# A decoder trunk in fp32 on one core: six seven-product pairs per feed-forward duo, and low parts of two down units by accumulating DMA

## The chip, the core and the metric

The kernel runs on one core of a Trainium2 chip. Its engines each work off a list of their own in order: PE (the matmul engine, with PEld loading its stationary operand), DVE, ACT, POOL and SP, and DMA queues move data between HBM and the on-chip memory. Engines wait for each other by semaphores. The metric is the device time of one launch in microseconds. The kernel before takes 2178.19 us, the median of three runs (2178.04 to 2179.07). Below, "us" is microseconds, and L followed by a number is a line of kernel.py; "before" and "changed" differ in line numbers, since the change adds lines (L294 and L296, the two halves of a split, become L314 and L316; L317 becomes L348; L423 becomes L469; L370 to L372 become L416 to L418; L445 to L447 become L491 to L493; L1129, L1133 and L1203 become L1179, L1183 and L1254).

## The reference

The reference is a two-layer decoder: a gated linear attention mixer, a feed-forward, a shared K/V projection, a differential attention and a second feed-forward, all in float32 on x of 256 tokens by 2048. The change touches the feed-forward alone, which runs twice with D_FF = 5632:

```python
def swiglu(h, w_gate_up, w_down):
    gate, up = jnp.split(h @ w_gate_up, 2, axis=-1)
    return (jax.nn.silu(gate) * up) @ w_down

f = swiglu(rmsnorm(x, pre_ffn_g[i]), ffn_w_gate_up[i], ffn_w_down[i])
x = x + rmsnorm(f, post_ffn_g[i])
```

## The kernel before, in words

**Float32 by three products.** Every weight streams in once, in units of 128 x 1024 floats (512 KB), by DMAs on SP's queue into five buffers called `raw`. A unit is then split into two parts that TensorE multiplies at its fast rate: ACT casts it to `hi` (L294), and DVE subtracts, `lo = raw - hi` (L296). Activations are held as such pairs too. A product of two 128 x 128 by 128 x 512 blocks is three matmuls of 128 x 512: high by high, high by the weight's low, low by the weight's high (`mm_act`, L370 to L372, and `triple`, L445 to L447). There are nine pairs of `hi` and `lo` buffers. A `raw` buffer comes free once its unit is split, and the next load then starts.

**The feed-forward.** Gate and up have 11 chunks of 512 columns each. Gate chunk c is worked together with up chunk 11 + c, as a "duo": eight steps over the contraction (s = 0 to 7), each of which brings four 128 x 512 blocks of weights for two contraction tiles, times two blocks of tokens, so eight products. For some steps the kernel uses a scheme with seven products in place of eight (a "seven-product pair" below), after Strassen: sums of the weights' blocks and of the activations' blocks are multiplied, and the duo's results are put together from seven PSUM banks. Its price is four additions of the raw weights on DVE (`sums`, L317), after which three whole units (kinds a, b, c) and one half unit (kind d, in narrow buffers) are split. An "ordinary pair" splits two units. The tuple FAST_FFN names the steps with seven products: (0, 2, 3, 4, 6); duo 1 uses (0, 2, 4, 6); chunk 0 runs without any.

After the last seven-product step of a duo, `early` takes four banks apart (a copy on ACT, L1140, and four operations on DVE, L1129); at step 7 `late` adds the remaining banks, applies silu on ACT (L1151) and multiplies gate by up on DVE (L1133). The gated chunk is transposed on PE and split again (`split_T`, L609 to L612) before the down projection can use it.

**The down runs.** The down projection works on groups of chunks, FF_GROUPS = ((0, 1), (2, 3), (4, 5), (6, 7), (8,), (9, 10)). After a duo comes a run of eight down units (four contraction steps for two column chunks), each of 12 matmuls; group (2, 3) for example gives one run for output chunks 0 and 1 after duo 3, and one for 2 and 3 after duo 4. A run starts its PSUM banks from the sum so far (a copy on ACT, L423), and a finished bank is copied back by ACT (`evac`, L1203). These copies stand in ACT's list among the casts.

**What sets the order.** The code asks for units in the order of a stream; `pump` converts units ahead of the step that takes them, as far as the buffers allow. A scheduler then orders each engine's list by its own estimate of times, unless an `issue_after` or a priority tells it otherwise.

Of the kernel before, what the change touches and what calls it, by code (L numbers as in the profile page):

```python
# [11 lines left out]
F32 = mybir.dt.float32  # L12
# [10 lines left out]
C = 512  # L23
# [16 lines left out]
FAST_MIX = (0, 2, 4, 6)  # L40
FAST_FFN = (0, 2, 3, 4, 6)
FAST_SECOND = (0, 2, 4, 6)
FAST_OUT = (0, 2, 3, 5)
FAST_V = (0, 2, 4, 5)
SKEW, LAST_SKEW = 7, 8
CHAIN = (3, 4, 5, 6)
FIRST_X = {1: [(1, 0), (0, 1)], 3: [(1, 1)], 5: [(0, 2)], 7: [(1, 2)], 9: [(0, 3)], 11: [(1, 3)]}
NRAW, NRING = 5, 9
V_BEGIN, V_EVERY, V_Q = 16, 3, 1


def ffn_pairs(c):

    return FAST_SECOND if c == 1 else FAST_FFN

# [78 lines left out]


def load_list(stream):
    out = []
    for name, idx, kind in stream:
        if kind in ("plain", "beside"):
            out.append((name, idx))  # L140
        elif kind == "a":
            out.extend((name, (n, idx[2])) for name, n in idx[:2])
    return out
# [43 lines left out]
class Trunk:  # L187
    def __init__(self, ctx, tc, t):
        self.ctx, self.tc, self.nc, self.t = ctx, tc, tc.nc, t

        def pool(name, **kw):
            return ctx.enter_context(tc.tile_pool(name=name, bufs=1, **kw))

        self.const = pool("const")
        self.big = pool("big")
        self.ring = pool("ring")
        self.hs = pool("hs")
        self.psum = pool("psum", space=bass.MemoryType.PSUM)
        self.dram = pool("dram", space=bass.MemoryType.DRAM)
        self.n = 0  # L200
        self.later = []
        self.stream = weight_stream()
        self.loads = load_list(self.stream)
        self.n_used = self.n_done = 0
        self.subs = {}
        self.raws = {}
        self.n_dma = self.n_conv = self.n_take = self.n_free = 0
        self.pool_lo = set()
        self.n_narrow = 0
        self.cap = 2  # L210
        self.ident = self.const.tile([P, P], F32, tag="ident", name="ident")
# [78 lines left out]
    def split(self, src, gp=False):  # L290
        nc = self.nc
        w = src.shape[-1]
        hi, lo = self.places(w)
        nc.scalar.copy(hi, src)  # L294
        eng = nc.gpsimd if gp else nc.vector
        eng.tensor_tensor(out=lo, in0=src, in1=hi.bitcast(F32), op=ALU.subtract)  # L296
        return hi, lo
# [27 lines left out]
    def convert(self):  # L325
# [3 lines left out]
        if kind == "plain":  # L329
            self.subs[n] = self.split(self.raw(), n in self.pool_lo) if n else self.split_halves(self.raw())  # L330
        elif kind == "beside":
# [17 lines left out]
    def take(self, name, idx, kind="plain"):  # L349
# [3 lines left out]
        self.pump()  # L353
        return self.subs.pop(n)

    def free(self):
# [92 lines left out]
    def duo_act(self, aT, forms, fast, c1, c2, early, late):  # L449

        ps = [self.acc() for _ in range(6)] + [self.tp().rearrange("p j t -> p (j t)")]
        for s in range(8):
            k1, k2 = 2 * s, 2 * s + 1
            if s in fast:
# [18 lines left out]
                if last:  # L473
                    early(ps)
                continue
            for (w, n), pair in ((c1, ((1, 0), (3, 1))), (c2, ((4, 1), (2, 2)))):
                wp = self.take(w, (n, s))
                for bank, which in pair:
# [3 lines left out]
                    if s == 7:  # L482
                        late(bank, ps)
                    if bank in (2, 3):
# [3 lines left out]
    def duo_apart(self, aT, forms, fast, chunks, early, late):  # L488
# [9 lines left out]
        for s in range(8):  # L498
            k1, k2 = 2 * s, 2 * s + 1
            if s not in fast:  # L500
                for (w, n), banks in zip(chunks, ((1, 3), (2, 7))):
                    wp = self.take(w, (n, s))
                    for b, bank in enumerate(banks):
# [4 lines left out]
                        if s == 7:  # L508
                            late(bank, ps)
                        self.tick()  # L510
# [15 lines left out]
            if last:  # L526
                early(ps)

# [631 lines left out]
    def ffn(self, fp, hT, rs, gi, wgu, wd, post, after, name, reload, side=None):  # L1160
        nc = self.nc
        self.narrow, self.n_narrow = (fp, 0, 3), 0
        forms = Forms(FAST_FFN, range(8), self.whole(4, [P, 4, 2, 4, P], f"{name}_fast", F32R))
# [9 lines left out]
        def gate_T(sg, c):  # L1173
# [3 lines left out]
            for b in range(2):  # L1177
                self.split_T(gTs[grp], 4 * grp.index(c), sg[:, b, :], b)

# [35 lines left out]
        for n, (kind, which, *chunks) in enumerate(plan):  # L1215
# [21 lines left out]
            def done(c, b, ps, grp=which):  # L1237
                (self.urgent(evac) if skew else evac)(grp, c, b, ps)

# [347 lines left out]
```

## Time and profile before

| | before |
|---|---|
| runs, median (lowest to highest) | 2178.19 us (2178.04 to 2179.07) |
| the profiled execution, its own time | 2178.21 us |
| its span, first to last instruction | 2176.5 us |
| PE busy | 2161.2 us (99%), 10098 matmuls |
| DVE busy | 1889.5 us (87%) |
| ACT busy | 1341.4 us (62%) |
| POOL busy | 36.3 us (2%) |
| DMA | 440.09 MB, mean 202 GB/s |
| mean granted TensorE clock | 0.999 |

The profile is of one execution. Its busy rows give each engine's busy time over the whole span; a row of a group of instructions reads "line, engine, operation, out<-in, shapes, count | busy us, mean ns of one | idle time of the engine just before them, and what ended most of it". A row of the timeline reads "start us, duration us, engine, line, operation, ...", with a wait in brackets. A row of the table of waits reads "engine, what it was about to write, its line <- the engine and line that released it: us in all, times, the longest". A matmul's own duration (0.39 us) overlaps the next one's, so its price is read from the distance between starts.

### The profile page before, as it was taken

What the parts mean: (1) busy time and instruction counts of PE and PEld (TensorE: products, weight loads), DVE (VectorE), ACT (ScalarE), POOL (GpSimd) and SP (SyncE); (2) the same over time, 40 slices, a digit from 0 to 9 for tenths busy, and PEclk for the clock granted to TensorE, in tenths of its full rate; (3) what the DMA queues carried; (4) which work ended last, traced back from release to release, by engine and by line L of the source; (5) the groups of instructions that cost most, each with busy time, mean ns of one, the idle gap of its engine ahead of it and who ended that gap; (6) DMA issues with size and microseconds to landing.
All of it is one profiled execution on the core that took longest, in us unless ns stands there. A gap on an engine that the chain in (4) does not pass through costs nothing.

```text
span 2176.5 us, 28464 instructions
## 1 busy us (share of the span) xinstructions
PE 2161.2 (99%) x10098; PEld 1797.6 (83%) x10098; DVE 1889.5 (87%) x2566; ACT 1341.4 (62%) x1888; POOL 36.3 (2%) x66
## 2 busy tenths in 40 slices
PE   9999999999999999999999999999999999999998
PEld 7887788888888888888788888888888888888886
DVE  7989988999899989988798567889998999899985
ACT  8656655666656666666676455556566666666664
POOL 1000000000000000000000000000000000000000
PEclk9999999999999999999999999999999999999999
DMA  8546566667655566565757655465656556566664
GB/s 309 168 150 191 176 228 212 215 212 246 204 179 193 198 213 212 195 222 191 239 189 245 189 172 164 149 233 195 230 197 221 189 178 197 204 209 220 204 212 136
DMA packets 123315, 440.09 MB, mean 202 GB/s; under 512 B 13899, under 2 KB 16628, under 8 KB 121380
## 3 DMA queue, kind: packets, MB, share of 16 engines
q1 hardware_dynamic: 121996, 436.44, 60.2%
q10 hardware_dynamic: 1176, 1.84, 0.2%
q8 instruction: 79, 1.29, 0.2%
q14 instruction: 64, 0.52, 0.1%
HBM read 429.82 MB, written 9.97 MB: 202 GB/s over the span
## 4 chain that ended last, share of the span: by engine, by line
PE 98%; DVE 1%; issue 0%; DMA 0%; ACT 0%; POOL 0%; SPq 0%; DVEq 0%; POOLq 0%; ACTq 0%
PE acc L445 13%; PE acc L447 13%; PE acc L446 13%; PE acc L372 11%; PE acc L370 11%; PE acc L371 11%; PE acc L588 8%; PE acc L589 4%; PE tp L445 3%; PE tp L446 3%; PE tp L447 3%; PE tp L609 1%; DVE lo L296 1%; PE acc L1310 0%; PE acc L1349 0%; PE tp L644 0%
## 5 line engine op out<-in xcount | busy, mean ns | idle before, releaser
L294 ACT CAST hi<-raw 128x1024 fp32r<-128x1024 f32 x905 | 929.7, 1051 | 568.2 <-DVE raw L317 227.2
L296 DVE TENSOR_TENSOR lo<-raw,hi 128x1024 fp32r<-128x1024 f32 x903 | 1079.6, 1219 | 182.2 <-ACT hi L294 179.4
L371 PE MATMUL acc<-lo,f_ffn_gT 128*128 128x512 f32 x704 | 273.7, 389 | 0.0
L370 PE MATMUL acc<-hi,f_ffn_gT 128*128 128x512 f32 x704 | 273.1, 390 | 0.0
L372 PE MATMUL acc<-hi,f_ffn_gT 128*128 128x512 f32 x704 | 268.5, 389 | 0.0
L445 PE MATMUL acc<-hi,h_ffn 128*128 128x512 f32 x666 | 259.3, 389 | 0.0
L447 PE MATMUL acc<-hi,h_ffn 128*128 128x512 f32 x666 | 259.3, 389 | 0.0
L446 PE MATMUL acc<-lo,h_ffn 128*128 128x512 f32 x666 | 259.1, 389 | 0.0
L372 PEld LDWEIGHTS acc<-hi,f_ffn_gT 128*128 128x128 f32 x704 | 132.2, 188 | 27.4
L370 PEld LDWEIGHTS acc<-hi,f_ffn_gT 128*128 128x128 f32 x704 | 132.0, 188 | 27.5 <-issue 0.6
L371 PEld LDWEIGHTS acc<-lo,f_ffn_gT 128*128 128x128 f32 x704 | 132.2, 188 | 27.1
L447 PEld LDWEIGHTS acc<-hi,h_ffn 128*128 128x128 f32 x666 | 125.0, 188 | 26.0
L446 PEld LDWEIGHTS acc<-lo,h_ffn 128*128 128x128 f32 x666 | 125.1, 188 | 25.9
L445 PEld LDWEIGHTS acc<-hi,h_ffn 128*128 128x128 f32 x666 | 125.0, 188 | 25.8
L588 PE MATMUL acc<-h_q,hi 128*128 128x512 f32 x256 | 92.6, 402 | 0.0
L588 PE MATMUL acc<-h_kv,hi 128*128 128x512 f32 x256 | 90.6, 399 | 0.0
L588 PE MATMUL acc<-h_mix,hi 128*128 128x512 f32 x256 | 90.6, 398 | 0.0
L317 DVE TENSOR_TENSOR raw<-sum,raw 128x512 f32<-128x512 f32 x122 | 84.3, 691 | 3.8
L317 DVE TENSOR_TENSOR raw<-raw 128x512 f32<-128x512 f32 x122 | 84.3, 691 | 3.6
L317 DVE TENSOR_TENSOR raw<-raw,raw 128x512 f32<-128x512 f32 x122 | 83.9, 687 | 2.3
L1203 ACT COPY f_ffn<-acc 128x512 f32<-128x512 f32 x80 | 46.9, 586 | 60.8 <-PE acc L372 60.6
L317 DVE TENSOR_TENSOR sum<-raw,raw 128x512 f32<-128x512 f32 x122 | 83.4, 684 | 0.0
(412 smaller groups left out, 3966.1 us busy)
## 6 DMA issues: line engine op xcount, KB each, us to landing
raw<-in_w_gu_dram SPq DMA_DIRECT2D x352, 512.0 KB, 4.5
raw<-in_w_d_dram SPq DMA_DIRECT2D x176, 512.0 KB, 4.9
raw<-in_gla_w_r_dram SPq DMA_DIRECT2D x32, 512.0 KB, 4.7
raw<-in_gla_w_v_dram SPq DMA_DIRECT2D x32, 512.0 KB, 4.0
raw<-in_gla_w_out_dram SPq DMA_DIRECT2D x32, 512.0 KB, 4.5
raw<-in_w_v_dram SPq DMA_DIRECT2D x32, 512.0 KB, 4.5
raw<-in_w_k_dram SPq DMA_DIRECT2D x32, 512.0 KB, 4.5
raw<-in_diff_w_q_dram SPq DMA_DIRECT2D x32, 512.0 KB, 4.2
```

Source lines behind the costliest of these rows:

```text
L294: nc.scalar.copy(hi, src)
L296: eng.tensor_tensor(out=lo, in0=src, in1=hi.bitcast(F32), op=ALU.subtract)
L317: nc.vector.tensor_tensor(out=out, in0=in0, in1=in1, op=ALU.add)
L370: nc.tensor.matmul(ps, ah, rh, start=(kt == 0 and not onto), stop=False, skip_group_check=onto)
L371: nc.tensor.matmul(ps, ah, rl, start=False, stop=False, skip_group_check=onto)
L372: nc.tensor.matmul(ps, al, rh, start=False, stop=(kt == 2 * ns - 1), skip_group_check=onto)
L445: nc.tensor.matmul(ps, ah, wh, start=first, stop=False)
L446: nc.tensor.matmul(ps, ah, wl, start=False, stop=False)
L447: nc.tensor.matmul(ps, al, wh, start=False, stop=last)
L588: nc.tensor.matmul(ps, lh, aT.both(kt), start=(kt == 0), stop=False)
L589: nc.tensor.matmul(ps[:, SEQ:], ll, aT.hi(kt), start=False, stop=(kt == KT - 1))
L1203: nc.scalar.copy(fc, ps)
```

## The change

Three things change in the feed-forwards.

- Steps with seven products: duos 2 to 9 get six of them, (0, 2, 3, 4, 5, 6); duo 10 keeps five, now (0, 2, 3, 5, 6); duo 1 keeps four. The forms of the activations for the sixth are built with the others, and half units now have two narrow buffers of their own and two places beside the activations' forms, where they had three such places.
- In each run of eight down units, units 6 and 7 are split without DVE: ACT writes the negated unit into `lo`, a DMA issued by POOL loads the unit from HBM once more and adds it to what stands in `lo`, and ACT casts `hi`. The buffer `lo` is of the same rounded type as `hi`, so that what ACT writes there is the negated high part, and the sum is the low part, raw - hi. There are 22 such units in each feed-forward.
- `early` and `late` of a duo are ordered, by the context manager `behind`, after the cast and the subtraction of the last unit that is converted up to three ahead of the one being taken.

```diff
-FAST_FFN = (0, 2, 3, 4, 6)
+FAST_FFN = (0, 2, 3, 4, 5, 6)
 FAST_SECOND = (0, 2, 4, 6)
+FAST_LAST = (0, 2, 3, 5, 6)
...
+DOWN_LO_BY_DMA, DUO_LO_BY_DMA = (6, 7), ()
+EARLY_BEHIND, LATE_BEHIND, DOWN_BEHIND, GATE_BEHIND = 3, 3, 0, 0
...
-    return FAST_SECOND if c == 1 else FAST_FFN
+    return FAST_SECOND if c == 1 else FAST_LAST if c == 10 else FAST_FFN
...
+def lo_by_dma(stream):
+
+    out, last, run = set(), None, 0
+    for n, (name, idx, kind) in enumerate(stream):
+        run = run + 1 if (name, kind) == last else 0
+        last = name, kind
+        if kind != "plain":
+            continue
+        if name in ("w_d0", "w_d1") and run % 8 in DOWN_LO_BY_DMA:
+            out.add(n)
...
+        cast = nc.scalar.copy(hi, src)
+        eng = nc.gpsimd if gp else nc.vector
+        rest = eng.tensor_tensor(out=lo, in0=src, in1=hi.bitcast(F32), op=ALU.subtract)
+        if not gp:
+            self.parts[self.n_conv] = cast.ins, rest.ins
+        return hi, lo
+
+    def split_by_dma(self, src, name, idx):
+
+        nc = self.nc
+        hi, lo = self.places(2 * C)
+        nc.scalar.activation(lo, src, AF.Copy, scale=-1.0)
+        nc.gpsimd.dma_start(lo, self.t[name][idx], accum_op=ALU.add)
         nc.scalar.copy(hi, src)
-        eng = nc.gpsimd if gp else nc.vector
-        eng.tensor_tensor(out=lo, in0=src, in1=hi.bitcast(F32), op=ALU.subtract)
         return hi, lo
...
+            if n in self.dma_lo:
+                self.subs[n] = self.split_by_dma(self.raw(), name, idx)
...
+    @contextmanager
+    def behind(self, ahead):
+
+        made = [n for n in self.parts if n < self.n_take + ahead]
+        if not made or not ahead:
+            yield
+            return
+        cast, rest = self.parts[max(made)]
+        with self.tc.issue_after(cast), self.tc.issue_after(rest):
+            yield
...
                 if last:
-                    early(ps)
+                    with self.behind(EARLY_BEHIND):
+                        early(ps)
...
                         if s == 7:
-                            late(bank, ps)
+                            with self.behind(LATE_BEHIND):
+                                late(bank, ps)
...
-        self.narrow, self.n_narrow = (fp, 0, 3), 0
+        self.narrow, self.n_narrow = (fp, 2, 2), 0
```

The scheduler reorders the lists around this. Three places show it, all of the first feed-forward; numbers behind names count up as the program is built. The first is DVE's list at the end of duo 5 and the start of the run of down units behind it. `lo_6384` and `lo_6396` before, `lo_6471` and `lo_6483` in the change, are the two units of the duo's last ordinary pair; the rows behind them are the run's units, and L1129 (L1179) is `early` and `late`. Before:

```order
L296 TENSOR_TENSOR lo_6441<-raw_6367,hi_6440 128x1024
L296 TENSOR_TENSOR lo_6453<-raw_6387,hi_6452 128x1024
L296 TENSOR_TENSOR lo_6465<-raw_6399,hi_6464 128x1024
L296 TENSOR_TENSOR lo_6477<-raw_6408,hi_6476 128x1024
L1129 TENSOR_TENSOR hs_6492<-acc_6234,sg_6491 128x512
L296 TENSOR_TENSOR lo_6486<-raw_6426,hi_6485 128x1024
L1129 TENSOR_TENSOR sg_6491<-tp_6203,hs_6492 128x512
L1129 TENSOR_TENSOR sg_6491<-acc_6182,sg_6491 128x512
```

In the change:

```order
L316 TENSOR_TENSOR lo_6471<-raw_6367,hi_6470 128x1024
L316 TENSOR_TENSOR lo_6483<-raw_6401,hi_6482 128x1024
L316 TENSOR_TENSOR lo_6495<-raw_6413,hi_6494 128x1024
L1179 TENSOR_TENSOR hs_6568<-acc_6297,sg_6567 128x512
L316 TENSOR_TENSOR lo_6507<-raw_6445,hi_6506 128x1024
L1179 TENSOR_TENSOR sg_6567<-tp_6266,hs_6568 128x512
L316 TENSOR_TENSOR lo_6516<-raw_6457,hi_6515 128x1024
L1179 TENSOR_TENSOR sg_6567<-acc_6245,sg_6567 128x512
L316 TENSOR_TENSOR lo_6528<-raw_6474,hi_6527 128x1024
L1179 TENSOR_TENSOR hs_6569<-acc_6278,sg_6567 128x512
```

Before, six units of the run are split ahead of the first operation of `early` (`lo_6405` to `lo_6477`); in the change one is (`lo_6495`), and the four operations stand between the splits of the next ones.

The second place is ACT's list, at the last units of that run and, further on, at the copies of the finished down sums. Before:

```order
L294 CAST hi_6513<-raw_6444 128x1024
L1151 ACTIVATE sg_6491<-sg_6491,rs_ffn_0_3744 128x512
L423 COPY acc_6600<-f_ffn_4427 128x512
L294 CAST hi_6535<-raw_6456 128x1024
...
L294 CAST hi_6668<-raw_6517 128x1024
L1203 COPY f_ffn_4427<-acc_6541 128x512
L294 CAST f_ffn_rest<-sum_6684 128x512
L294 CAST hi_6689<-raw_6566 128x1024
L1203 COPY f_ffn_4427<-acc_6542 128x512
L294 CAST hi_6709<-raw_6517 128x1024
```

In the change:

```order
L325 ACTIVATE lo_6561<-raw_6510 128x1024
L327 CAST hi_6560<-raw_6510 128x1024
L469 COPY acc_6678<-f_ffn_4440 128x512
L325 ACTIVATE lo_6590<-raw_6519 128x1024
L327 CAST hi_6589<-raw_6519 128x1024
L314 CAST hi_6612<-raw_6531 128x1024
...
L314 CAST hi_6747<-raw_6594 128x1024
L1254 COPY f_ffn_4440<-acc_6618 128x512
L1254 COPY f_ffn_4440<-acc_6677 128x512
L1254 COPY f_ffn_4440<-acc_6619 128x512
L314 CAST hi_6768<-raw_6643 128x1024
L314 CAST hi_6802<-sum_6763 128x512
```

Units 6 and 7 of the run (`raw_6510`, `raw_6519`) have two rows each where a unit had one, and `hi_6612` is the first cast of the next duo. `hi_6689` before and `hi_6768` in the change are the same unit, kind b of the next duo's pair 2: one copy of a down sum stands ahead of it before, three stand ahead of it now.

The third place is PE's list in duo 6, at step 5 (names in `f_ffn_rest` are the activations' forms of the later pairs). Before it is an ordinary pair, and the three matmuls of a product stand in a row:

```order
L445 MATMUL acc_6719<-hi_6837,h_ffn_1_3490 128x512
L446 MATMUL acc_6719<-lo_6838,h_ffn_1_3490 128x512
L447 MATMUL acc_6719<-hi_6837,h_ffn_1_3490 128x512
L445 MATMUL acc_6741<-hi_6837,h_ffn_1_3490 128x512
L446 MATMUL acc_6741<-lo_6838,h_ffn_1_3490 128x512
L447 MATMUL acc_6741<-hi_6837,h_ffn_1_3490 128x512
```

In the change it is a seven-product pair, and several matmuls with `hi` stand ahead of the first with `lo`:

```order
L491 MATMUL tp_6806<-hi_6933,f_ffn_rest 128x512
L491 MATMUL acc_6810<-hi_6933,f_ffn_rest 128x512
L491 MATMUL acc_6837<-hi_6957,f_ffn_rest 128x512
L492 MATMUL tp_6806<-lo_6934,f_ffn_rest 128x512
L493 MATMUL tp_6806<-hi_6933,f_ffn_rest 128x512
L492 MATMUL acc_6810<-lo_6934,f_ffn_rest 128x512
L493 MATMUL acc_6810<-hi_6933,f_ffn_rest 128x512
```

The step has 21 matmuls where it had 24. The scheduler's order also differs in the steps around it; each unit's `hi` is asked for a few matmuls earlier than its `lo`.

More of the change, by code (lines that the diff above doesn't have):

```diff
@@ L1 @@
 import math
-from contextlib import ExitStack
+from contextlib import ExitStack, contextmanager
 import numpy as np
@@ L133, in weight_stream @@
     return out
+def lo_by_dma(stream):
[7 more added lines that the diff above has]
+            out.add(n)
+        if name in ("w_gu0", "w_gu1") and idx[0] % 11 > 1 and idx[1] in DUO_LO_BY_DMA:
+            out.add(n)
+    return out
 def load_list(stream):
@@ L205, in __init__ @@
         self.subs = {}
+        self.parts = {}
         self.raws = {}
@@ L208, in __init__ @@
         self.pool_lo = set()
+        self.dma_lo = lo_by_dma(self.stream)
         self.n_narrow = 0
@@ L329, in convert @@
         if kind == "plain":
-            self.subs[n] = self.split(self.raw(), n in self.pool_lo) if n else self.split_halves(self.raw())
+            name, idx, _ = self.stream[n]
+            if n in self.dma_lo:
+                self.subs[n] = self.split_by_dma(self.raw(), name, idx)
+            else:
+                self.subs[n] = self.split(self.raw(), n in self.pool_lo) if n else self.split_halves(self.raw())
         elif kind == "beside":
@@ L508, in duo_apart @@
                         if s == 7:
-                            late(bank, ps)
+                            with self.behind(LATE_BEHIND):
+                                late(bank, ps)
                         self.tick()
@@ L526, in duo_apart @@
             if last:
-                early(ps)
+                with self.behind(EARLY_BEHIND):
+                    early(ps)
     def rest_of(self, forms, i, name):
@@ L1177, in gate_T @@
             for b in range(2):
-                self.split_T(gTs[grp], 4 * grp.index(c), sg[:, b, :], b)
+                with self.behind(GATE_BEHIND):
+                    self.split_T(gTs[grp], 4 * grp.index(c), sg[:, b, :], b)
         def new_sg():
@@ L1237, in done @@
             def done(c, b, ps, grp=which):
-                (self.urgent(evac) if skew else evac)(grp, c, b, ps)
+                if skew:
+                    self.urgent(evac)(grp, c, b, ps)
+                else:
+                    with self.behind(DOWN_BEHIND):
+                        evac(grp, c, b, ps)
             base = None if which == first else part
```

## The prediction

> **What bounds the kernel now.** I read the page's busy shares and its chain first, then the waits of PE, then a busy table over one repeating stretch of the feed-forward, then that stretch row by row.
>
> ```profile
> PE 2161.2 (99%) x10098; PEld 1797.6 (83%) x10098; DVE 1889.5 (87%) x2566; ACT 1341.4 (62%) x1888; POOL 36.3 (2%) x66
> ...
> PE 98%; DVE 1%; issue 0%; DMA 0%; ACT 0%; POOL 0%; SPq 0%; DVEq 0%; POOLq 0%; ACTq 0%
> ```
> ```profile
> PE acc L372 <- DVE h_kv L650: 2.8, 2, 2.3
> ```
> ```profile
> 560.62:686.17 125.55, 125.55 (x565) 104.17 (x563) 114.56 (x132) 78.01 (x95) 0.00 (x0) 1.00 0.61 201
> 686.17:811.72 125.55, 125.55 (x564) 104.17 (x563) 114.45 (x132) 78.03 (x95) 0.00 (x0) 1.00 0.60 201
> ```
> The chain is PE for 98% of the span, and the longest entry in the list of PE's waits is 2.8 us, outside the feed-forward. The two windows (stretch, us, then busy us of PE, weight load, DVE, ACT, POOL) are two periods of one feed-forward, each of two duos and two runs of eight down units: PE is busy for all of each 125.55 us at a granted clock of 1.00, so matmuls alone set the time. DVE is the next engine: 114.45 of 125.55 us, 11.1 us idle per period, 5.5 us per duo with its run.
>
> A busy PE may be waiting on nothing and still run below its peak, so the price of a matmul is read from starts:
>
> ```profile
> 708.20 0.39 PE L446 MATMUL acc<-lo,f_ffn_fast 128*128 128x512 f32 x1
> 708.43 0.39 PE L447 MATMUL acc<-hi,f_ffn_fast 128*128 128x512 f32 x1
> 708.65 0.39 PE L445 MATMUL acc<-hi,h_ffn 128*128 128x512 f32 x1
> 708.88 0.39 PE L446 MATMUL acc<-lo,h_ffn 128*128 128x512 f32 x1
> ```
> Three steps in 0.68 us: 0.2267 us per matmul. A product of three matmuls costs 0.68 us, a seven-product pair 4.76, an ordinary pair 8 x 0.68 = 5.44, a down unit (12 matmuls) 2.72.
>
> **What the change removes from PE.** Eight duos in each of two feed-forwards get one more seven-product pair, each with one product less: 16 x 3 = 48 matmuls, 48 x 0.2267 = 10.9 us. It is all on the path that sets the end, as long as the operands arrive. That condition is the whole question, because it is DVE that pays.
>
> **What it adds to DVE.** The price of a pair on DVE, from starts where DVE has no gap:
>
> ```profile
> 688.80 0.68 DVE L317 TENSOR_TENSOR raw<-raw,raw 128x512 f32<-128x512 f32 x1
> ...
> 695.58 0.69 DVE L317 TENSOR_TENSOR raw<-raw,raw 128x512 f32<-128x512 f32 x1
> ...
> 699.98 4.62 DVE L296 TENSOR_TENSOR lo<-raw,hi 128x1024 fp32r<-128x1024 f32 x4
> ...
> 709.05 5.76 DVE L296 TENSOR_TENSOR lo<-raw,hi 128x1024 fp32r<-128x1024 f32 x5
> ```
> From the first sum of one seven-product pair to that of the next, 695.58 - 688.80 = 6.78 us: four sums, three splits of a whole unit, one of a half. Five splits in a row take 5.76 us, 1.15 each, so an ordinary pair costs 2.3. One pair converted adds 4.5 us. In the down run two of eight units lose their split: -2.3. Net +2.2 us per duo with its run: 57.2 (half of 114.45) becomes 59.4 us, while PE's 62.8 becomes 62.1. The margin shrinks from 5.5 to 2.7 us. Over the program that is 16 x 4.5 - 44 x 1.15 = +21 us of DVE (44 units, 22 in each feed-forward), and some 5 us for the two sixth forms, in the first chunks, where all units are ordinary. DVE would be 96% used in a period, so the average fits; the lead within the duo has to be looked at.
>
> **The lead.** In a seven-product pair PE gains 6.78 - 4.76 = 2.02 us on DVE, in an ordinary pair DVE gains 5.44 - 2.3 = 3.1, in a down unit 1.57. The split at 699.98 (the last whole one of pair 4, over at 701.20) is read at 708.20: a lead of 7.0 us. The one at 709.05 (pair 6, over at about 710.3) is first read here:
>
> ```profile
> 718.40 0.39 PE L446 MATMUL acc<-lo,f_ffn_rest 128*128 128x512 f32 x1
> ```
> a lead of 8.1. With pair 5 converted, this second lead falls by 3.1 + 2.02 to 3.0 us if DVE comes into the duo as far ahead as now, and the two spared splits could add 2.3: at best 5.3. At worst DVE comes in later. What limits its lead at the duo's start is ACT, in order:
>
> ```profile
> 744.43 0.59 ACT L1203 COPY f_ffn<-acc 128x512 f32<-128x512 f32 x1 [4.34 <-PE acc L372]
> ```
> A copy of a finished down sum stands between the casts for the next pairs and waits 4.34 us for PE; DVE waits behind it. In the new order three such copies stand ahead of the casts of pair 2 in one kind of run and two in the other. Counting matmuls in the new order from the duo's last ordinary pair, PE ends the last of these sums at 29.0 or 28.1 us; copy, cast and split (0.59, 1.05, 1.22, and 0.35 I allow for signals) bring pair 2's second unit to 32.2 or 31.3, and PE reads it at 40.8 or 38.7: a lead of 8.6 or 7.4. From there to the same unit of pair 6 PE takes 19.5 or 21.5 us (60.27 less these; the new order runs some first matmuls ahead of the low part's), DVE 4 x 6.78 = 27.1, and 1.3 more for a gate's split in the second kind. Left: 1.0 or 0.5 us. I go by this end, since ACT's order is what the row shows, and the reckoning is good to about 1.2 us. So a duo in four may wait, about 0.2 us each on the mean: 16 x 0.2 = 3 us. If DVE's cover is gone altogether, it is the second rival.
>
> **The evacuations** move behind the first down unit's split. DVE's four operations of some 0.6 us then stand among the splits of the run, where DVE now has gaps; the sums that PE needs for the run's first chunks are freed by the first of them. Nothing, while the lead holds; up to 0.6 us per run if a sum comes late. This is inside the 1.2 us.
>
> **The low parts by DMA.**
>
> ```profile
> L294 ACT CAST hi<-raw 128x1024 fp32r<-128x1024 f32 x59 | 60.6, 1050 | 36.9 <-DVE raw L317 25.3 <-DMA raw<-in_w_d_dram 6.0 <-issue 2.6
> ```
> ```profile
> raw<-in_w_d_dram SPq DMA_DIRECT2D x176, 512.0 KB, 4.9
> ```
> ACT gets a negated copy per unit (priced as its cast, 1.05), 2.1 us per run, and with the converted pair 1.05 + 0.62 more: 39.0 of 62.8 us becomes 42.8 of 62.1. It stays off the path. POOL issues 44 DMAs, where it has nothing queued in these stages; the norms' small operations behind the last two come after PE's last sums anyway. The DMA engines are busy 0.60 and get 44 x 0.52 = 23 MB on 440. The trace has no accumulating DMA. Below, it costs a plain load, 4.9 us; above, twice that with the destination read, plus the issue on POOL, about 11. What it may take: unit 6's own load follows the release by unit 1's split (about 3 us into the last pair), lands 4.9 later, so the negated copy ends near 9 to 10; PE first reads the low part at 20.1 or 22.9 by the count. About 10 us are free, so I price it at nothing, with the upper end just touching.
>
> [...]
>
> **Sum.** The profiled execution took 2178.21 us (span 2176.5, 1.7 around it), as good as the median of 2178.19. 2178.2 - 10.9 = 2167.3; + 3 for thin leads = **2170 us**.
>
> **Rivals.** (1) *Part of the gain is eaten by DVE*: the lead runs out in every duo, by 0.3 to 0.9 us, 5 to 14 us in all: 2172 to 2181, say 2175. For it: the lead of 0.5 to 1.0. Against: DVE's gaps of now (8.9 us a period are waits for casts) shrink when it is late.
>
> ```profile
> DVE lo L296 <- ACT hi L294: 8.9, 13, 1.8
> ```
> (2) *DVE becomes the bound*, slower than before. If DVE keeps all of its 5.5 us of gaps per duo, it needs 59.4 + 5.5 = 64.9 us, 2.1 over the present 62.8: 16 x 2.1 = +34, 2212; it decides above 3.4 us of gaps, half way 2195. For: the four ACT operations of the two units stand ahead of the next duo's first cast. Against: gaps that come from waiting for PE go when PE is not behind. (3) *The accumulating DMA lands late*, above some 10 us from the negated copy: each microsecond more costs one in each of 22 runs; at 12 us 2170 + 44 = 2214. [...] (4) *The saving is not there*: PE's removed products turn into waits of the same size, 2176 to 2180. Nothing in the present order shows why it should come out even.
>
> **Chances.** Forecast (2166 to 2172) 0.56, rival 1 0.24, rival 2 0.09, rival 3 0.08, rival 4 0.03. Rounds of this kernel tell about 0.2%, 4.4 us, from no change: 2173.8 to 2182.6. Faster: the forecast and a third of rival 1, 0.64; the same: the rest of it and rival 4, 0.19; slower 0.17. Range 2166 (all of the 10.9 and a little from the tail) to 2184, where rivals 2 and 3 are left out. The likeliest case's own range is 2166 to 2172.
>
> **What would show it.** 10050 matmuls; PE idle under 0.5 us in each duo; a period of 124.2 us, plus what is waited for, where now 125.55 stands; DVE busy about 118.8 in it; POOL's DMAs landing under 10 us after issue. PE waiting on DVE's split in pairs 5 and 6 means rival 1; DVE at over 98% of a longer period, rival 2; PE waiting for a DMA into the low part at the seventh unit of a run, rival 3. The forecast is wrong where the period is above 125.2.

## The result, and the profile after

The change takes 2184.96 us, the median of seven runs (2178.57 to 2191.51), beside 2178.49 us before (seven runs, 2178.04 to 2179.07). The ratio is 1.003, 95% interval 1.0015 to 1.0044: slower by about 6.5 us, where 2170 was forecast with a range up to 2184. Its runs also spread over 13 us where the kernel before spreads over 1.

The page of the profiled execution (2184.96 us, span 2183.2), in the order of the page: busy times, two DMA queues (packets, MB, share of 16 engines), the chain:

```profile
PE 2159.4 (99%) x10050; PEld 1790.8 (82%) x10050; DVE 1910.5 (88%) x2630; ACT 1394.8 (64%) x1966; POOL 76.2 (3%) x110
...
q1 hardware_dynamic: 121996, 436.44, 59.6%
q0 software_dynamic: 6336, 23.07, 5.8%
...
PE 74%; DVE 12%; issue 6%; DMA 5%; ACT 2%; SPq 0%; POOL 0%; DVEq 0%; POOLq 0%; ACTq 0%
```

The 48 matmuls are gone (10050), DVE has 21 us more, and PE is still "99%" busy; but only 74% of the chain that ended last is PE, where it was 98%. The other thing to see is the second queue: 23 MB of accumulating DMAs cost 5.8% of the DMA engines' time, the 436 MB of plain loads 59.6%, so a byte that is added took 1.84 times the engine time of a byte of the plain loads.

PE's waits, the longest entries of each (us in all, times, longest):

```profile
PE acc L418 <- DVE h_kv L700: 3.9, 1, 3.9
PE acc L809 <- DMA hs<-in_onehot_dram: 2.3, 1, 2.3
...
PE acc L417 <- DMA lo<-in_w_d_dram: 1.3, 2, 0.7
PE acc L416 <- ACT acc L469: 1.0, 1, 1.0
PE acc L416 <- ACT f_ffn_gT L661: 0.8, 1, 0.8
```

The first is the start of the K/V projection, the second a small table (the one-hot rows for the position bias) loaded in the first down run. No entry is long; to find where the time went, the same matmuls are looked up in both timelines. Before:

```profile
482.74 0.81 PE L759 MATMUL acc<-hs,tab 33*8 33x384 f32 x2
...
1087.75 0.49 PE L372 MATMUL acc<-hi,h_kv 128*128 128x512 f32 x1 [2.27 <-DVE h_kv L650]
...
1470.47 0.50 PE L372 MATMUL acc<-hi,h_ffn 128*128 128x512 f32 x1 [0.31 <-DVE h_ffn L650]
...
2167.53 0.39 PE L372 MATMUL acc<-hi,f_ffn_gT 128*128 128x512 f32 x1
```

After:

```profile
485.90 0.81 PE L809 MATMUL acc<-hs,tab 33*8 33x384 f32 x2 [2.33 <-DMA hs<-in_onehot_dram]
...
1093.41 0.80 PE L418 MATMUL acc<-hi,h_kv 128*128 128x512 f32 x1 [3.86 <-DVE h_kv L700]
...
1477.77 0.50 PE L418 MATMUL acc<-hi,h_ffn 128*128 128x512 f32 x1 [0.31 <-DVE h_ffn L700]
...
2173.88 0.39 PE L418 MATMUL acc<-hi,f_ffn_gT 128*128 128x512 f32 x1
```

The one-hot matmul comes 3.16 us later than before. From there to the K/V wait the distance grows by 2.50 us although 24 matmuls (5.44 us) are gone from the first feed-forward: 7.9 us are lost in it. To the second feed-forward 1.64 us more, and in it (5.44 us of matmuls gone, 0.95 us shorter) 4.5 us. With 0.3 us behind the last matmul: 3.2 + 7.9 + 1.6 + 4.5 + 0.3 = 17.5 us lost against 10.9 us saved, which is, but for rounding, the 6.7 us between the spans.

Part of the loss is no wait at all. The table by windows (stretch, us, busy PE, weight load, DVE, ACT, POOL, then the granted clock, DMA share, GB/s) right behind the two long waits:

```profile
484.00:487.70 3.70, 1.80 (x7) 0.98 (x8) 2.04 (x4) 1.20 (x2) 0.00 (x0) 1.00 0.72 251
487.70:491.10 3.40, 3.40 (x10) 2.63 (x9) 1.97 (x3) 1.04 (x1) 0.00 (x0) 0.50 0.45 135
...
1091.80:1098.60 6.80, 5.19 (x12) 4.14 (x13) 6.80 (x18) 4.69 (x11) 0.55 (x1) 0.50 1.01 341
```

For 3.4 us behind the first and 6.8 us from within the second, the granted clock is 0.50. PE was busy for 3.4 and 5.2 us of these, and its matmuls started 0.43 us apart (488.08 to 490.64) where they start 0.23 apart at full clock; by the granted clock half of that, an estimate of 4.3 us, is lost. The profile counts PE as busy in it.

### The profile page after: what moved, and what is told of

It is laid out like the page before. It is cut to its first block, busy times and chain, and to the rows that moved or that the text cites. A ratio compares the mean times of both kernels' runs of the same rounds, so it can differ in the third digit from the quotient of the medians.

```text
span 2183.2 us, 28625 instructions
## 1 busy us (share of the span) xinstructions
PE 2159.4 (99%) x10050; PEld 1790.8 (82%) x10050; DVE 1910.5 (88%) x2630; ACT 1394.8 (64%) x1966; POOL 76.2 (3%) x110
## 3 DMA queue, kind: packets, MB, share of 16 engines
q1 hardware_dynamic: 121996, 436.44, 59.6%
q10 hardware_dynamic: 1176, 1.84, 0.2%
## 4 chain that ended last, share of the span: by engine, by line
PE 74%; DVE 12%; issue 6%; DMA 5%; ACT 2%; SPq 0%; POOL 0%; DVEq 0%; POOLq 0%; ACTq 0%
PE acc L492 9%; PE acc L493 9%; PE acc L491 9%; PE acc L418 9%; PE acc L416 9%; PE acc L417 9%; PE acc L638 8%; DVE lo L316 6%; PE acc L639 4%; DVE raw L348 3%; DMA raw<-in_w_d_dram 2%; PE tp L492 2%; PE tp L493 2%; PE tp L491 2%; DMA raw<-in_w_gu_dram 1%
## 5 line engine op out<-in xcount | busy, mean ns | idle before, releaser
L314 ACT CAST hi<-raw 128x1024 fp32r<-128x1024 f32 x877 | 899.8, 1051 | 556.8 <-DVE raw L348 226.2
L316 DVE TENSOR_TENSOR lo<-raw,hi 128x1024 fp32r<-128x1024 f32 x875 | 1045.9, 1220 | 168.0 <-ACT hi L314 165.8
L492 PE MATMUL acc<-lo,h_ffn 128*128 128x512 f32 x618 | 241.1, 390 | 0.0
L493 PE MATMUL acc<-hi,h_ffn 128*128 128x512 f32 x618 | 240.6, 390 | 0.0
L491 PE MATMUL acc<-hi,h_ffn 128*128 128x512 f32 x618 | 231.1, 389 | 0.0
L491 PEld LDWEIGHTS acc<-hi,h_ffn 128*128 128x128 f32 x618 | 116.2, 188 | 24.1
L493 PEld LDWEIGHTS acc<-hi,h_ffn 128*128 128x128 f32 x618 | 116.0, 188 | 23.9
L348 DVE TENSOR_TENSOR raw<-raw 128x512 f32<-128x512 f32 x138 | 95.4, 691 | 4.2
L348 DVE TENSOR_TENSOR raw<-sum,raw 128x512 f32<-128x512 f32 x138 | 95.3, 691 | 4.1
L348 DVE TENSOR_TENSOR raw<-raw,raw 128x512 f32<-128x512 f32 x138 | 95.1, 689 | 2.9
L348 DVE TENSOR_TENSOR sum<-raw,raw 128x512 f32<-128x512 f32 x138 | 94.4, 684 | 0.0
L326 POOL DMA_DIRECT2D lo<-in_w_d_dram x44 | 38.7, 880 | 1292.0 <-ACT lo L325 719.4
```

Of the source, the lines that this page charges most:

```text
L314: cast = nc.scalar.copy(hi, src)
L316: rest = eng.tensor_tensor(out=lo, in0=src, in1=hi.bitcast(F32), op=ALU.subtract)
L326: nc.gpsimd.dma_start(lo, self.t[name][idx], accum_op=ALU.add)
L348: nc.vector.tensor_tensor(out=out, in0=in0, in1=in1, op=ALU.add)
L491: nc.tensor.matmul(ps, ah, wh, start=first, stop=False)
L492: nc.tensor.matmul(ps, ah, wl, start=False, stop=False)
```

## The experiments

All times are medians; "before" was run beside each on the same chip and took 2178.7 to 2179.2 us. The theories as they stood in the expectations: **A**, the accumulating DMAs hold the DMA engines and make small loads late at two places; **B**, all of the loss is DVE's thin margin; **C**, the spared splits are not needed; **D** (formed after the first two rounds), the adding makes plain loads late as well, ACT's casts wait for them, and what stands behind the casts waits too.

| run | what it is | us (lowest to highest) | ratio to before, 95% |
|---|---|---|---|
| e1_pairs_only | the change, no DMAs | 2184.67 (2182.01 to 2185.35) | 1.0026, 1.0016 to 1.0035 |
| e2_dma_only | before, with the DMAs | 2183.47 (2182.45 to 2184.24) | 1.0020, 1.0011 to 1.0029 |
| e3_no_behind | the change, evacuations not held back | 2190.09 (2185.58 to 2195.04) | 1.0052, 1.0039 to 1.0065 |
| e4_no_edge_dma | the change, 32 DMAs of 44 | 2179.72 (2175.85 to 2182.11) | 1.0003, 0.9994 to 1.0012 |
| e5_plain_copy | the change, copying in place of adding | 2169.99 (2169.69 to 2171.32) | 0.9960, 0.9947 to 0.9972 |
| e6_onehot_early | the change, one-hot table early | 2182.56 (2177.73 to 2186.74) | 1.0016, 1.0008 to 1.0025 |
| e7_both_early | and the last gain early | 2180.81 (2176.63 to 2184.01) | 1.0004, 0.9995 to 1.0013 |
| e8_both_units57 | and units 5, 7 | 2182.54 (2177.23 to 2186.56) | 1.0015, 1.0006 to 1.0024 |
| e9_pool_67 | the change, low parts on POOL | 2187.51 (2185.57 to 2189.82) | 1.0045, 1.0032 to 1.0059 |
| e10_dma_7 | the change, unit 7 alone by DMA | 2174.16 (2171.35 to 2177.08) | 0.9979, 0.9970 to 0.9987 |
| e11_dma_7_both_early | and both loads early | 2175.63 (2172.95 to 2177.67) | 0.9983, 0.9975 to 0.9992 |
| e12_change_again | the change itself | 2183.67 (2180.51 to 2188.06) | 1.0023, 1.0013 to 1.0034 |
| e13_plain_twice | e5 with each copy twice | 2175.70 (2172.89 to 2178.17) | 0.9986, 0.9977 to 0.9995 |
| e14_plain_7 | e10, copying in place of adding | 2171.58 (2171.17 to 2172.24) | 0.9967, 0.9955 to 0.9980 |

### The two halves of the change apart

```diff
-DOWN_LO_BY_DMA, DUO_LO_BY_DMA = (6, 7), ()
+DOWN_LO_BY_DMA, DUO_LO_BY_DMA = (), ()
```

> The change without the accumulating DMAs: all 44 units are split by DVE again, everything else stays. Theory A (the accumulating DMAs hold the DMA engines and make small loads late at two places, about 8 us of the changed kernel's time with the half clock behind them; the rest are thin leads on DVE): the waits for the one-hot load and for the last gains go back to what they were before, 0 and about 2.5 us, but DVE gets 2.3 us more per duo with its run, 61.7 of 62.1 us, so PE waits for DVE's splits in nearly every duo: 2185 to 2200 us. Theory B (all of the loss is DVE's margin): the same direction, but at least as much worse as the DVE work added, 22 x 2.3 = 51 us of it, less what gaps are left: above 2200 us. Theory C (the spared splits are not needed): about 2176, faster than the change.

It took 2184.67, just below A's range. Theories B and C are out: 44 splits more on DVE cost far less than 51 us, but they do cost the whole gain. PE waits for DVE's splits at six places and for the gate's transposed parts at seven:

```profile
PE acc L416 <- ACT f_ffn_gT L661: 3.8, 7, 1.8
PE acc L418 <- DVE h_kv L700: 3.6, 1, 3.6
PE tp L492 <- DVE lo L316: 1.5, 6, 0.2
```

The K/V wait is as long as in the change although no DMA adds here, so that wait has more than one cause.

```diff
-FAST_FFN = (0, 2, 3, 4, 5, 6)
+FAST_FFN = (0, 2, 3, 4, 6)
-FAST_LAST = (0, 2, 3, 5, 6)
+FAST_LAST = (0, 2, 3, 4, 6)
-EARLY_BEHIND, LATE_BEHIND, DOWN_BEHIND, GATE_BEHIND = 3, 3, 0, 0
+EARLY_BEHIND, LATE_BEHIND, DOWN_BEHIND, GATE_BEHIND = 0, 0, 0, 0
-        self.narrow, self.n_narrow = (fp, 2, 2), 0
+        self.narrow, self.n_narrow = (fp, 0, 3), 0
```

> The kernel before with the accumulating DMAs alone (five seven-product pairs, no late evacuations, the half units' places as before). PE has as many matmuls as before and DVE 2.3 us less work per run, so no lead gets thinner. Theory A: the DMAs alone cost what they cost in the change, 2.3 us of waiting for the one-hot load with 1.7 us of half clock behind it, some 4 us at the start of the K/V projection, and 1 to 2 us of waiting for low parts: 2183 to 2188 us, and a wider spread than before. Theory B: no cost where DVE has margin, 2178.

2183.47, 4.7 us above before, as A said: the DMAs cost time even where DVE has room, at the two places and hardly anywhere else (in the profile a K/V wait of 3.9 us with 3.4 us at half clock behind it, and a one-hot wait of 1.2 us; no wait for a low part, which A had at 1 to 2 us). The spread stayed at 1.8 us, so A's wider spread did not come.

```diff
-EARLY_BEHIND, LATE_BEHIND, DOWN_BEHIND, GATE_BEHIND = 3, 3, 0, 0
+EARLY_BEHIND, LATE_BEHIND, DOWN_BEHIND, GATE_BEHIND = 0, 0, 0, 0
```

> The change without the rule that orders a duo's evacuation behind splits. Theory A and B alike leave the two edges as they are; it tells what the order of the evacuations is worth inside the feed-forward. If the late evacuations cause the waits for gate parts and PSUM banks (4 waits of 0.8 to 1.0 us in the changed kernel), these go: 2180. If they protect the splits, DVE's splits come later and PE waits in most duos: 2190 or more.

2190.09, within the second forecast, so the order that puts the evacuations behind splits is worth some 5 us in the medians; the ranges overlap widely. That it is the splits which it protects is not shown: in the profile, that of the fastest of the five runs (2185.58), PE waits at eleven places for ACT's casts (3.3 us) and at none listed for a split of the feed-forward.

### The two places

```diff
-        if name in ("w_d0", "w_d1") and run % 8 in DOWN_LO_BY_DMA:
+        if name in ("w_d0", "w_d1") and run % 8 in DOWN_LO_BY_DMA and idx[1] < 18 and idx not in ((1, 2), (1, 3)):
```

> The change with 16 accumulating DMAs per feed-forward instead of 22: none in the first run of down units (where the one-hot table is loaded) and none in the last two (where the last gains are loaded and the next stage begins). Theory A: the two stalls go with the half clock behind them, about 8 us: 2176 to 2178, with the spread of before. Theory B (or another cause of the two stalls): 2184 or more, since 12 more splits are on DVE.

2179.72, above A's range: 4 to 5 us of the 8 came back, and the spread did not go (6 us). The one-hot wait was gone; the K/V projection still began with waits of 1.2 and 2.7 us.

```diff
-        oh = self.scratch()[: REL_BUCKETS + 1, :384]
+        oh = self.narrow[0].tile([P, C], F32, tag="early", name="onehot", bufs=1)[: REL_BUCKETS + 1, :384]
```

> The change with the one-hot table loaded early, into a buffer of its own, and nothing else moved on purpose. Theory A: the stall of 2.3 us in the first down run goes, and the 1.7 us of half clock behind it where there was one: 2181 to 2182.5. If that wait only hid another one behind it (low parts, pair 2), 2184.

> The same, and the gain of the last output chunk is loaded early too (the buffer is free again by then). Theory A: DVE's last product with the gain no longer waits 2.25 us for the load, so the K/V projection's first wait is back to some 2.5 us or less and its half clock is shorter or gone: 2 to 4 us below the run with the one-hot table alone, 2177 to 2180. If the order of DVE's splits ahead of the K/V operands sets that wait, it stays at 3.5 to 4 us, and the time within 1 us of the other run.

The second adds this:

```diff
                 if chunks[0] == 0:
                     reload()
+                    gains[3] = fp.tile([P, C], F32, tag="early", name=self.uid("gain"), bufs=1)
+                    nc.sync.dma_start(gains[3], post[:, 3 * C :].partition_broadcast(P))
```

2182.56 and 2180.81, each a little above A's range. The runs of each spread over 7 to 9 us, so a single step is not clear of the noise. The K/V wait is back to 2.2 us in the second; but together the two bring 3 to 4 us of the 15 that e5 shows below, and the waits for low parts grew to 4.5 us in that profile. Loading the two early does not give the loss back.

```diff
-DOWN_LO_BY_DMA, DUO_LO_BY_DMA = (6, 7), ()
+DOWN_LO_BY_DMA, DUO_LO_BY_DMA = (5, 7), ()
```

> The same again, with units 5 and 7 of each run by accumulating DMA instead of 6 and 7. If two such DMAs in a row (2.7 us apart) make each other late, they land earlier when apart (7 instead of 9 us) and the waits for low parts go: 1 to 2 us faster than the run with both loads early. If it is the single DMA's own time, unit 5 is read 2.7 us earlier than unit 6 and waits more: 1 to 5 us slower.

2182.54, no better than with units 6 and 7 (2180.81): apart by another unit, the two DMAs landed in 9.0 us in place of 9.7, and not in 7.

### Copying in place of adding

```diff
-        nc.gpsimd.dma_start(lo, self.t[name][idx], accum_op=ALU.add)
+        nc.gpsimd.dma_start(lo, self.t[name][idx])
```

> The change with a plain copy in place of each accumulating DMA (same queue, place and size; the low parts of the 44 units then hold the whole weight, so the sums are not the reference's). Theory A1 (it is the adding that keeps the DMA engines busy nearly twice as long per byte, 5.8% for 23 MB against 59.6% for 436 MB): landing falls from 9.3 us to 5 or 6, the waits for low parts and for the one-hot table go, with the half clock behind the latter: 2178 to 2181. Theory A2 (any second load of the unit does it): landing and time as in the change, 2184 to 2185.

2169.99, with a spread of 1.6 us. PE's, DVE's, ACT's and POOL's lists are the same as the change's, row by row; only the kind of transfer differs, and with it the values in those low parts. It is the forecast time, and 15 us under the change (14 under its second round, e12). So A1 has the right suspect, but gave it too small a price, though the landing fell only to 7.6 us and not to 5 or 6: all of what the change lost beyond the forecast hangs on the adding. The page's queue row, and ACT's waits for loads (us in all, times, longest):

```profile
q0 software_dynamic: 6336, 23.07, 3.3%
```
```profile
ACT hi L314 <- DMA raw<-in_w_d_dram: 47.2, 70, 2.5
...
ACT hi L314 <- DMA raw<-in_w_gu_dram: 7.1, 10, 1.4
```

The change, by the same view:

```profile
ACT hi L314 <- DMA raw<-in_w_d_dram: 49.3, 69, 2.8
...
ACT hi L314 <- DMA raw<-in_w_gu_dram: 31.5, 22, 2.8
```

ACT's casts wait 31.5 us for gate and up units, with copies 7.1, before 4.6; for down units the waits hardly differ. One place shows how a late load, there of a down unit, reaches PE. ACT in the change, in the run of down units behind duo 10 of the first feed-forward:

```profile
1053.24 1.05 ACT L314 CAST hi<-raw 128x1024 fp32r<-128x1024 f32 x1 [1.79 <-DMA raw<-in_w_d_dram]
1057.06 1.05 ACT L314 CAST hi<-raw 128x1024 fp32r<-128x1024 f32 x1 [2.77 <-DMA raw<-in_w_d_dram]
1058.02 0.58 ACT L661 CAST f_ffn_gT<-tp 128x512 fp32r<-128x512 f32 x1
```

The cast of the gate's transposed part (L661) had its operand since PE's transposes of 1052.43 and 1054.49; it stands behind two casts that wait for plain loads, and PE waits 0.80 us for it at 1058.65. The second of these loads was issued right behind the split that freed its buffer (1043.58 to 1044.81). A row of the chain (start, us, what) shows how long it took, where half of the down units' loads take 4.8 us or less:

```profile
1044.83 12.13 DMA raw<-in_w_d_dram
```

And the DMA engines in these microseconds (the last two columns are DMA share and GB/s; the accumulating DMAs were issued at 1043.85 and 1046.88):

```profile
1043.80:1047.80 4.00, 4.00 (x19) 3.32 (x18) 3.54 (x5) 4.00 (x6) 1.78 (x2) 1.00 0.86 228
1047.80:1051.80 4.00, 4.00 (x20) 3.30 (x19) 2.68 (x3) 3.66 (x6) 0.00 (x0) 1.00 1.01 242
1051.80:1055.80 4.00, 4.00 (x23) 3.35 (x22) 1.66 (x2) 1.05 (x1) 0.00 (x0) 1.00 1.04 279
1055.80:1059.80 4.00, 3.20 (x14) 2.31 (x14) 1.65 (x2) 2.74 (x4) 0.00 (x0) 1.00 1.01 406
```

All 16 engines are busy for 12 us, at 242 to 279 GB/s while they add and 406 when they copy again. With copies the same run has two such windows, at 365 and 399:

```profile
1039.20:1043.20 4.00, 4.00 (x19) 3.30 (x18) 2.84 (x4) 4.00 (x7) 0.00 (x0) 1.00 1.02 365
1043.20:1047.20 4.00, 4.00 (x23) 3.36 (x22) 2.15 (x3) 2.10 (x3) 0.00 (x0) 1.00 1.03 399
```

A part of that could be read before. The same table of the kernel before, at the end of a duo and in the run behind it:

```profile
712.00:716.00 4.00, 4.00 (x19) 3.30 (x19) 2.82 (x4) 2.10 (x2) 0.00 (x0) 1.00 0.92 282
716.00:720.00 4.00, 4.00 (x20) 3.30 (x19) 3.15 (x3) 3.33 (x5) 0.00 (x0) 1.00 0.97 388
720.00:724.00 4.00, 4.00 (x19) 3.34 (x18) 3.75 (x5) 3.16 (x4) 0.00 (x0) 1.00 0.98 349
724.00:728.00 4.00, 4.00 (x20) 3.30 (x19) 4.00 (x7) 2.99 (x6) 0.00 (x0) 1.00 0.79 281
728.00:732.00 4.00, 4.00 (x19) 3.30 (x18) 4.00 (x6) 0.61 (x1) 0.00 (x0) 1.00 0.48 137
732.00:736.00 4.00, 4.00 (x20) 3.28 (x19) 3.93 (x7) 3.09 (x4) 0.00 (x0) 1.00 0.00 0
```

The mean share of 0.60 is made of stretches at 0.98 and stretches at 0. ACT casts the run's units 6 and 7 at 720.7 and 723.2 here, so DMAs behind these casts would have met 0.98, 0.79 and 0.48 in the twelve us from 720 on: room for 3.0 us of all 16 engines (the four us behind are empty). An estimate from the queue rows: a copied unit takes 1.6 us of all 16 engines (3.3% of 2168.0 us for 44), an added one 2.9 (5.8% of 2183.2 us for 44). Two copies, 3.3 us, about fit into that room; two added units, 5.8 us, do not.

### Another way to the low parts, and half as many

```diff
-        self.dma_lo = lo_by_dma(self.stream)
+        self.dma_lo = set()
+        self.pool_lo = lo_by_dma(self.stream)
```

> The change with the low parts of units 6 and 7 subtracted by POOL (one operation on the chip, from the unit that is loaded already) in place of the accumulating DMA and ACT's negated copy. POOL's subtraction of such a unit took 2.4 us twice at the start of the kernel before, and POOL is idle in the feed-forward. Theory D (the loss is the adding DMAs' time on the DMA engines, which makes plain loads late, on which ACT's casts wait): no extra load, so the time of the plain copy or better, 2168 to 2172. Rival: POOL and DVE hinder each other when both read two operands on the chip: DVE's splits beside a POOL subtraction take longer than 1.22 us and the leads go, 2178 to 2190.

2187.51: the rival. The timelines of DVE and of POOL in one run:

```profile
603.81 1.23 DVE L317 TENSOR_TENSOR lo<-raw,hi 128x1024 fp32r<-128x1024 f32 x1 [0.34 <-ACT hi L315]
604.96 3.54 DVE L1184 SCALAR_TENSOR_TENSOR sg<-hs,rs_ffn,sg 128x512 f32<-128x512 f32 x2
```
```profile
601.35 5.95 POOL L317 TENSOR_TENSOR lo<-raw,hi 128x1024 fp32r<-128x1024 f32 x2 [58.49 <-ACT hi L315]
```

Two operations of `late` that took 1.40 us in a row before take 3.54: they end 1.2 us behind POOL's two subtractions (607.3), and these take 5.95 us where two at 2.40 would take 4.8. Over the program the longest split is 3491 ns, where it is 1229 before, and POOL's mean is 2610 ns in place of 2398. So each has rows that took longer beside the other; what they contend for is not shown. The casts' waits for gate and up units fell to 5.7 us, as D said, and it did not help.

```diff
-DOWN_LO_BY_DMA, DUO_LO_BY_DMA = (6, 7), ()
+DOWN_LO_BY_DMA, DUO_LO_BY_DMA = (7,), ()
```

> The change with an accumulating DMA for unit 7 alone; unit 6 is split by DVE. Theory D: half the adding, so the late loads are fewer than half; DVE has 1.15 us more per run, 60.5 of 62.1. With the plain copies at 2170 and no DMA at all at 2184.7, a lead that runs out steeply gives 2180 or more, a lead that still holds gives 2172 to 2178.

2174.16: faster than before by 0.2% and than the change by 0.5%, the best of those that leave nothing out. ACT's waits for gate and up units are at 9.0 us, and PE waits for no split of the feed-forward in its profile, so DVE's lead holds with one spared split:

```profile
ACT hi L314 <- DMA raw<-in_w_gu_dram: 9.0, 10, 1.7
```

With both loads early as in e7:

> Unit 7 alone by accumulating DMA, and the one-hot table and the last gain loaded early. Theory D: the kernel with unit 7 alone took 2174.2 and still had a one-hot wait of 1.7 us with half a clock behind it; without these (3 us) and with a shorter K/V wait (0 to 2 us): 2169 to 2172, faster than the kernel before and than the change. If the stalls only move on to the next wait: 2173 to 2175.

2175.63, above both forecasts, and the ranges overlap: the early loads bring nothing here. The one-hot wait was gone, but the gate's transposed parts were waited for at seven places (2.4 us in all, against 1.4 us without the early loads), and a stretch of half clock stood at 491.5 us all the same.

> The change itself again, for a second profile. Theory D: the same kinds of waits at partly other places, ACT's casts waiting about 30 us for gate and up units, the one-hot wait of 2 us or more; 2182 to 2187, spread about 10 us. If the one-hot stall and the K/V stall belong to one execution alone, they are gone here.

2183.67, spread 7.6 us. The one-hot wait (3.0 us) and the K/V wait (3.1) are there again, and ACT waits 30.6 us for gate and up units. So these belong to the change and not to one execution.

Since PE's list is the same in the change, in e12 and with copies (e5), the start of each matmul can be set against the start of the same matmul with copies. That tells where the time goes (us more than with copies, rounded):

| where | change | e12 |
|---|---|---|
| ahead of the one-hot matmul | 1.1 | 0.4 |
| its wait, and half clock behind it | 4.0 | 3.1 |
| from there to the K/V projection's wait | 3.9 | 3.7 |
| that wait, and half clock behind it | 3.5 | 2.0 |
| from there to the end | 2.7 | 4.9 |
| sum | 15.2 | 14.0 |

The two places make up half of the loss in one profile and about a third in the other; the rest lies inside the two feed-forwards. In e12 a larger part of that is low parts that came late, which PE does not wait for with copies (us in all, times, longest):

```profile
PE acc L417 <- DMA lo<-in_w_d_dram: 3.6, 2, 2.1
```

One of the two, with its issue:

```profile
1816.90 0.88 POOL L326 DMA_DIRECT2D lo<-in_w_d_dram  x1 [60.21 <-ACT lo L325]
1827.43 0.50 PE L417 MATMUL acc<-lo,f_ffn_gT 128*128 128x512 f32 x1 [2.11 <-DMA lo<-in_w_d_dram]
```

PE asked for the low part 8.4 us behind its issue, at the other place of e12 7.6, at the two of the change 8.4; each is the seventh unit of its run.

### What in the adding costs so much

```diff
-        nc.gpsimd.dma_start(lo, self.t[name][idx], accum_op=ALU.add)
+        copy = nc.gpsimd.dma_start(lo, self.t[name][idx])
+        spare = self.uid("spare")
+        with self.tc.issue_after(copy.ins):
+            nc.gpsimd.dma_start(self.dram.tile([P, 2 * C], F32, tag=spare, name=spare), self.t[name][idx])
```

> The kernel with plain copies (2170.0, wrong low parts), with a second plain load of the same unit issued behind each, to a place in HBM that nothing reads. Theory D (engine time): the POOL queue's share rises from 3.3% to 6.5%, above the adding's 5.8%; plain loads behind come late as in the change (ACT's casts wait 25 us or more for gate and up units in place of 7), the one-hot wait is back: 2180 to 2186. Rival (only adding does it, by reading its destination or by its longer landing): 2170 to 2173.

2175.70, between the two. The DMA engines get what the adding takes, and the casts' waits come back:

```profile
q0 software_dynamic: 7744, 46.14, 5.9%
```
```profile
ACT hi L314 <- DMA raw<-in_w_gu_dram: 25.4, 27, 1.7
```

So time on the DMA engines, without any adding, costs 5.7 of the 15 us. The other 8 to 9 us need the adding itself, or its place. Most of them lie at the two places: the one-hot wait did not come back, against the expectation, the K/V wait is 2.1 us, and the clock is full throughout, where the change lost 7.5 and 5.1 us more than the copies there. Why the adding reaches these places and a second copy does not is not settled: the spare loads stand behind the copies, an addition holds up its own low part too (it lands in 9.3 us, the copies here in 7.9), and the scheduler's order is slightly different. Nor does the sum of the casts' waits tell the time: it is 25.4 us here, and 11.5 us in the profile of e8, which takes 2182.54.

> The kernel with unit 7 alone (2174.2), with a plain copy in place of the accumulating DMA (wrong low parts for these 22 units). If the 4 us that separate it from two plain copies (2170.0) are the adding: 2168 to 2171. If they are the lead that 1.15 us more of DVE work per run makes thinner: 2173 to 2175.

2171.58, between the two forecasts. With one unit per run the adding costs 2.6 us (2174.16 against 2171.58), with two it costs 14 to 15 (2183.67 and 2184.96 against 2169.99). One split more per run for DVE, with half as many copies, costs 1.6 us at most (2171.58 against 2169.99, the ranges overlap a little).

## Why the prediction was wrong, step by step

- **The price of a matmul and the 48 removed, 10.9 us: right.** With copies the kernel takes 2169.99 us: 2178.2 - 10.9 + 2.7. The period, from the transposition of one duo's gate to that of the second duo behind, was forecast at 124.2 us, with 125.2 as its limit. Three periods of the first feed-forward took 376.05 us in the change (564.55 to 940.60), 125.4 each, and 373.06 with copies (559.47 to 932.53), 124.4 each; in the second feed-forward it is 124.9 and 124.6.
- **The leads, 3 us: right in size as long as loads come in time, but partly by luck.** With copies (e5) 2.7 us are lost, yet PE waits for no split of the feed-forward in that profile; its list has 0.4 us for the gate's transposed parts, and the rest is in delays too short for the list. So the leads held better than reckoned. The two spared splits are what carries them: without these (e1) PE loses 14.7 us more. DVE's 1910.5 us are 21 more than before; the 5 us more for the two sixth forms do not show in this total.
- **The evacuations at nothing: an effect with the other sign.** Undoing their order costs some 5 us (e3), which the sum did not have.
- **The low parts by DMA at nothing: the step that failed.** Two things were wrong in it. The larger stands in "The DMA engines are busy 0.60 and get 44 x 0.52 = 23 MB on 440." That takes the mean share, and a byte that is added for a byte that is copied. By the estimate above, two added units need 5.8 us of all 16 engines where the trace before left about 3.0 in twelve us, and the change has shares of 1.01 to 1.04 for twelve us in the run shown. The adding pushes back the loads of the down units and of the next duo, the one-hot table and the last gains (DVE waits 6.7 us for gains, with copies 1.0, before not at all), and the lists of ACT and DVE carry it on to PE. The sum had no term for them; copying in place of adding puts it at 14 to 15 us, of which the engines' time alone brought 5.7 (e13); what makes up the rest of the adding's price stays open. The smaller is the low part's own landing: 9.3 us (5.4 to 11.7) is inside the bounds, but of the "about 10 us" free there were 7.6 to 8.4 at the places where PE waited, 1.3 us in all in the change and 3.6 in e12. The upper bound doubles a plain load for the reading of the destination, 2 x 4.9 = 9.8 us, and that comes near the 9.3 by luck: copies from the same queue landed in 7.6 us, not in 4.9, and the adding made that 1.2 times as long, not twice. That the reading of the destination makes the price was the author's estimate, and no run shows it.
- **The edges of the stage: not looked at.** 2.3 us of waiting at the one-hot matmul, 1.6 us more at the K/V projection, and 4.3 us at half clock behind these two waits, in the profiled execution. The prediction counted a wait as what it lasts.
- **Rival 1** (2172 to 2181) has two of the 15 runs of the change in its range, and its ground, DVE's lead, was not the cause: with copies DVE's list is the same and the lead holds. **Rival 2** would have had DVE above 98% of a period; these two windows show it at 115.79 and 118.21 of 125.55 us, with PE full or nearly:

```profile
560.62:686.17 125.55, 125.55 (x564) 103.97 (x563) 115.79 (x139) 82.15 (x101) 3.52 (x4) 1.00 0.69 218
686.17:811.72 125.55, 124.72 (x556) 102.39 (x555) 118.21 (x141) 83.42 (x103) 3.52 (x4) 1.00 0.69 218
```

- **Rival 3** was right in part. Its sign, PE waiting for a DMA into the low part at the seventh unit of a run, was there at two places in each profile and not in each of 22 runs; most of the harm is done by what the accumulating DMA keeps waiting. The factor of two in the upper bound comes near to the queue rows, 5.8% against 3.3% for the same bytes, 1.76 times; it should have been put to the DMA engines' time in the stretch rather than to the landing of one transfer.

## What to carry to other kernels

Before a transfer is priced at nothing, set its time on the DMA engines against the share that they have left in windows of a few microseconds where it will run; behind a mean of 0.60 there were windows of 0.98, and where the room did not do (5.8 us of engine time into about 3.0, by the estimate above), the loads behind it paid (ACT waited 31.5 us for gate and up units, with copies 7.1), with all that stood behind the engine that waited for them. A replacement for one engine's work is best tried in the smallest dose: one unit of eight by DMA gained 0.2%, two lost 0.3%. And to tell whether a suspect transfer matters, change its kind and leave the order alone: copying in place of adding gave the answer in one run.

## What the runs showed of the hardware that was not expected

- **Half clock behind short waits.** Stretches at a granted clock of 0.50 lasted 3.4 us, or 6.8, and began behind or within waits of 1.6 (0.7 and 0.9 close together, in e11) to 4.2 us. The wait does not decide alone: the K/V wait of 2.1 to 2.3 us had such a stretch behind it in e7, e10 and e14 and none in the kernel before, e5, e8, e11 and e13; the one-hot wait had one at 2.3 us in the change and none at 3.0 in its second profile. What starts a stretch and what sets its length is not shown. Waits shorter than the stretch had one behind them: in e7 PE was busy for 1.2 of the 3.4 us ahead of it (1086.8 to 1090.2).
- **The spread.** Kernels with two accumulating DMAs per run and six seven-product pairs spread over 6 to 13 us, with copies (five runs) over 1.6, and with the DMAs but five pairs over 1.8. Adding is not needed for a spread of nearly that size: with each copy twice (e13) it is 5.3. What differs from execution to execution is not shown.
- **A small load behind a full queue.** The one-hot table is 50 KB, and took 7.35 us from issue to use in the chain of the change, where the DMA share from 478 to 482 us is 1.07 (with copies 0.56, before 0.11):

```profile
478.51 7.35 DMA hs<-in_onehot_dram
```
